# Channel mixer up projection: three 256-column passes into one sum, in place of a 512-column and a 256-column pass

## The chip, the core and the metric

The kernel runs on one core of a Trainium2 chip. The time is the device time of one execution in microseconds; of the kernel before there are three runs, and their median is 1437.25 us (1434.41 to 1437.47). One more execution was recorded by the hardware profiler; the rows quoted below are from it. TensorE multiplies matrices, VectorE (DVE) and ScalarE (ACT) do elementwise work, GpSimd (POOL) some small operations, and the SyncE queue (SP) issues the transfers between HBM and the on-chip memory SBUF. Matmuls write to PSUM, from where VectorE and ScalarE read.

## The reference

One layer of a diffusion backbone works on 256 latent tokens of width 2048 (and 256 context tokens in its first half). After a token mixer with a gated residual comes the channel mixer, and its first half is what is changed here:

```python
def conv_ffn(h, w_up, cw, cb, w_down, grid):
    gate, val = jnp.split(h @ w_up, 2, axis=-1)
    if grid:
        gate = dwconv2d_grid(gate, cw, cb)
    ...
    return (jax.nn.gelu(gate, approximate=False) * val) @ w_down
```

`h` is 256 x 2048, `w_up` 2048 x 11264 (two halves of 5632), `dwconv2d_grid` a depthwise 3x3 convolution over a grid of 4 x 64 tokens. All of it is fp32.

## The kernel before

**Precision in parts.** TensorE is fed numbers in a reduced fp32 format. Each operand is therefore split into a rounded part (hi) and the rest (lo), and a product is summed from hi x hi, hi x lo and lo x hi. A weight block of 128 x 2048 goes through `wtile` (L130 to L141): a transfer into `raw` on the SP queue, a cast on ScalarE into `whi` (L137), and the difference on VectorE into `wlo` (L140). There are three buffers of `raw`, three of `whi`, two of `wlo`. `take` hands out the block that is ready and prepares the next one. The buffers of `whi` and `wlo` are 64 floats longer than a block, and a table `places` says at which float of its buffer each block's two parts start: WIDE 0 and 0, NARROW 16 and 16 (64 bytes), PAIRED 16 for hi and 0 for lo.

**Stages.** First come modulation and the value projection, then eight heads of the token mixer (blocks ff and fb with 512 columns, q, b and a with 256 columns, all through `gemm_w`), eight blocks g, the output projection (wo), the residual and the modulated activations `h2`; then `phase3`, the channel mixer's up stage, and `phase4`, its down projection (dn). In phase 3 there are NFF = 44 values of j; for each there is a gate block and a val block, 88 blocks in all. The weights are the stationary operand (128 x 128 at a time, 16 of them per block, index kb), and the activations are the moving one: `h2` is laid out as [128, 16, 2, 256], so that for each kb the 256 columns of hi and the 256 of lo lie side by side.

**A pair.** For each kb, `mm2_w` (L201 to L207) sends whi over all 512 columns at once: the left half of the PSUM tile gets hi x hi, the right half hi x lo. Then it sends wlo over the 256 columns of hi into the left half. The q, b, a and g blocks use `mm3_w` (L192 to L199) instead: three passes of 256 columns, all into one sum. The first gate block (`late`, L768) has three passes of 256 columns in another order, since parts of h2 become ready only then.

**Behind the matmuls.** `add_parts` (L1140 to L1144) copies the right half from PSUM to SBUF on ScalarE (`low`) and adds the left half on VectorE. For a gate block this gives `g`; ScalarE makes the centre tap and the bias from it (`gacc`, L1151), VectorE adds the eight other taps (L1157), ScalarE applies GELU (`ge`, L1161). For a val block the sum gives `hd`, which is multiplied by `ge` (L1137) and split into `hid_hi` (ScalarE) and `hid_lo` (VectorE, L989) for phase 4.

**Order.** TensorE's instructions stand in the order of the program; those of VectorE and ScalarE are placed by a scheduler by priorities, weights first.

Of the kernel before, what the change touches and what calls it, by code (L numbers as in the profile page):

```python
# [8 lines left out]
F32 = mybir.dt.float32  # L9
# [3 lines left out]
AF = mybir.ActivationFunctionType  # L13
PSUM = bass.MemoryType.PSUM

P = 128
D = 2048
SEQ = 256
DEPTH = 1
HEADS = 8  # L20
# [3 lines left out]
NFF = DFF // P  # L24
KB = D // P
# [17 lines left out]
Y_DG, Y_CX, Y_O, Y_OT, Y_CT = 22, 6.5, 1.5, 6.5, 6  # L43

WBUF = 2048 + 64
WIDE, NARROW, PAIRED = (0, 0), (16, 16), (16, 0)
LEVELS = (1, 2, 4, 8, 16, 32, 64)


# [64 lines left out]
class _Kernel:  # L114
# [83 lines left out]
        nc.tensor.matmul(out, wh, xl, start=False, stop=False)  # L198
        nc.tensor.matmul(out, wl, xh, start=False, stop=stop)  # L199

    def mm2_w(self, ps, hi, lo, x, kb, start, stop):  # L201


        nc = self.nc
        nc.tensor.matmul(ps, hi[:, kb * P:(kb + 1) * P], x, start=start, stop=False, skip_group_check=True)  # L205
        nc.tensor.matmul(ps[:, :SEQ], lo[:, kb * P:(kb + 1) * P], x[:, 0], start=False, stop=stop,  # L206
                         skip_group_check=True)  # L207

    def mm3_x(self, out, hi, lo, xh, xl, kb, start, stop, w=512, tick=True):

        nc = self.nc
        wh = hi[:, kb * w:(kb + 1) * w]
        wl = lo[:, kb * w:(kb + 1) * w]
        nc.tensor.matmul(out, xh, wh, start=start, stop=False)  # L214
        nc.tensor.matmul(out, xh, wl, start=False, stop=False)  # L215
        nc.tensor.matmul(out, xl, wh, start=False, stop=stop)  # L216
        if tick:
            self.tick(w * 3 / 2400)
# [30 lines left out]
    def run(self):  # L249
        tc, nc, a = self.tc, self.nc, self.a  # L250

        def enter(**kw):
            p = tc.tile_pool(**kw)
            return p, p.__enter__()
# [18 lines left out]
        for j in range(NFF):  # L273
            srcs += [a["wup"][0, j], a["wup"][1, j]]
        srcs += [a["wdn"][n, kq] for n in range(4) for kq in range(NFF // 4)]
        places = ([WIDE] * 2 + [NARROW] * 3) * HEADS + [NARROW] * HEADS + [WIDE] * 16 + [PAIRED] * 2 * NFF
        places += [WIDE] * NFF


# [62 lines left out]
        upp, up = enter(name="up", bufs=2, side="right")  # L342
# [412 lines left out]
            nc.scalar.copy(G[:, q * 512:(q + 1) * 512], ps)  # L755


    def gemm_w(self, key, x, n, paired=False, late=False):

        hi, lo = self.take()  # L760
        ps = self.mm_tile(key)
        wk = lambda w, kb: w[:, kb * P:(kb + 1) * P]
        if late:

            for q in range(KB // 4):
                for i, (w, part) in enumerate(((hi, 0), (lo, 0), (hi, 1))):
                    for kb in range(4 * q, 4 * q + 4):
                        self.nc.tensor.matmul(ps[:, part * SEQ:(part + 1) * SEQ], wk(w, kb), x[:, kb, part],  # L768
                                              start=kb == 0 and i == 0, stop=kb == KB - 1 and i > 0,
                                              skip_group_check=True)  # L770
            return ps
        for kb in range(KB):
            if paired:
                self.mm2_w(ps, hi, lo, x[:, kb], kb, kb == 0, kb == KB - 1)
            else:
                self.mm3_w(ps[:, :n], hi, lo, x[:, kb, 0, :n], x[:, kb, 1, :n], kb, kb == 0, kb == KB - 1)
            self.tick(n * 3 / 2400)
        return ps

# [349 lines left out]
    def phase3(self, up):  # L1129
        nc = self.nc  # L1130
        for j in range(NFF):
            ps = self.gemm_w("gate", self.h2, SEQ, True, j == 0)
            ge = self.gate_conv(up, j, ps)
            ps = self.gemm_w("val", self.h2, SEQ, True)
            hd = up.tile([P, SEQ], F32, tag="hd", name="hd")
            self.add_parts(up, hd, ps)
            nc.vector.tensor_mul(hd, hd, ge)  # L1137
            self.split(self.hid_hi[:, j, :], self.hid_lo[:, j, :], hd)

    def add_parts(self, up, out, ps):  # L1140

        low = up.tile([P, SEQ], F32, tag="low", name="low")
        self.nc.scalar.copy(low, ps[:, SEQ:])
        self.nc.vector.tensor_add(out, ps[:, :SEQ], low)  # L1144

    def gate_conv(self, up, j, ps):
        nc = self.nc
        g = up.tile([P, 4, 64], F32, tag="gate", name="gate")
        acc = up.tile([P, 4, 64], F32, tag="gacc3", name="gacc3")
        self.add_parts(up, g.rearrange("p r c -> p (r c)"), ps)  # L1150
        nc.scalar.activation(acc, g, AF.Identity, scale=self.par("fcw", j * 9 + 4), bias=self.par("fcb", j))  # L1151
        taps = [(dy, dx) for dy in (-1, 0, 1) for dx in (-1, 0, 1) if dy or dx]
        for dy, dx in taps:
            r0, r1 = max(0, -dy), min(4, 4 - dy)
            c0, c1 = max(0, -dx), min(64, 64 - dx)
            o = acc[:, r0:r1, c0:c1]
            nc.vector.scalar_tensor_tensor(o, g[:, r0 + dy:r1 + dy, c0 + dx:c1 + dx],  # L1157
                                           self.par("fcw", j * 9 + (dy + 1) * 3 + dx + 1), o,
                                           op0=ALU.mult, op1=ALU.add)
        ge = up.tile([P, SEQ], F32, tag="ge", name="ge")  # L1160
        nc.scalar.activation(ge, acc.rearrange("p r c -> p (r c)"), AF.Gelu)  # L1161
        return ge
# [134 lines left out]
```

## Time and profile before

| | |
|---|---|
| runs, median (three runs) | 1437.25 us (1434.41 to 1437.47) |
| the profiled execution | 1433.68 us |
| its span | 1431.9 us, mean granted clock 0.993 |
| TensorE busy | 1390.7 us (97%) |
| VectorE busy | 1097.4 us (77%) |
| ScalarE busy | 738.1 us (52%) |
| first matmul of the first gate block | 686.5 us |
| first matmul of the first val block | 692.6 us |
| first matmul of the down projection | 1179.8 us |

The table's last three lines bound the up stage: about 493 us of the span. In the profile, a group's row gives line, engine, operation, tiles (written <- read), shape and count, then busy time, the mean duration of one in ns, and idle time of the engine before it. PE stands for TensorE's matmuls, PEld for its weight loads. Matmuls overlap, so a duration isn't the distance from one to the next; that is read from starts in the timeline.

### The profile page before, as it was taken

The numbers are of one execution on the slowest core, as the hardware profiler recorded it, in microseconds if no ns is written. First come the engines' busy times: TensorE is split into PE (matmuls) and PEld (weight loads), VectorE is DVE, ScalarE is ACT, GpSimd is POOL, SyncE is SP. The second block draws the span as 40 slices with busy tenths as digits, with TensorE's granted clock in tenths as the row PEclk, the third lists the DMA queues.
The fourth block names the chain that finished last, engine by engine and source line by source line (L and its number), as shares of the span: only waits on it lengthen the run. The fifth ranks groups of instructions, "written<-read, shape, count | busy, mean of one in ns | idle before, by whom it ended". The sixth has DMA issues, their size and how long they took to land.

```text
span 1431.9 us, 22182 instructions
## 1 busy us (share of the span) xinstructions
PE 1390.7 (97%) x8880; PEld 1179.1 (82%) x8880; DVE 1097.4 (77%) x1665; ACT 738.1 (52%) x1218; POOL 31.2 (2%) x57
## 2 busy tenths in 40 slices
PE   4999999999999999999999999999999999999997
PEld 2566888888888898888888888888888888888886
DVE  3444898899999999776788888888888886667544
ACT  4334456766666676437654545545455543333531
POOL 0000001001000010000000000000000000000000
PEclk8999999999999999999999999999999999999999
DMA  9988676446654665786445545555455558878652
GB/s 370 386 322 332 252 267 232 169 173 224 231 194 160 236 231 216 288 299 260 146 178 191 191 179 195 185 189 194 177 195 187 186 196 311 332 273 318 236 188 105
DMA packets 49143, 329.21 MB, mean 230 GB/s; under 512 B 5392, under 2 KB 5648, under 8 KB 10896
## 3 DMA queue, kind: packets, MB, share of 16 engines
q1 hardware_dynamic: 49040, 327.80, 61.5%
q8 instruction: 69, 1.13, 0.3%
q14 instruction: 34, 0.28, 0.1%
HBM read 323.58 MB, written 4.19 MB: 229 GB/s over the span
## 4 chain that ended last, share of the span: by engine, by line
PE 79%; DVE 10%; ACT 4%; DMA 3%; issue 2%; POOL 1%; SPq 0%; DVEq 0%; POOLq 0%; ACTq 0%
PE val L205 11%; PE gate L205 11%; PE val L206 6%; PE gate L206 6%; PE dn L215 5%; PE dn L214 5%; PE dn L216 5%; DVE wlo L140 3%; PE v L214 2%; PE wo L216 2%; PE wo L214 2%; PE wo L215 2%; DVE acc L942 2%; PE v L216 2%; PE v L215 2%
## 5 line engine op out<-in xcount | busy, mean ns | idle before, releaser
L140 DVE TENSOR_TENSOR wlo<-raw,whi 128x2048 fp32r<-128x2048 f32 x193 | 441.6, 2288 | 104.5 <-PE dn L215 56.1
L137 ACT CAST whi<-raw 128x2048 fp32r<-128x2048 f32 x193 | 369.0, 1912 | 292.7 <-PE val L205 93.6
L205 PE MATMUL val<-h,whi 128*128 128x512 f32 x704 | 248.4, 395 | 0.0
L205 PE MATMUL gate<-h,whi 128*128 128x512 f32 x688 | 242.7, 395 | 0.0
L206 PE MATMUL val<-h,wlo 128*128 128x256 f32 x704 | 197.8, 281 | 0.0
L206 PE MATMUL gate<-h,wlo 128*128 128x256 f32 x688 | 193.3, 281 | 0.0
L1157 DVE SCALAR_TENSOR_TENSOR gacc<-gate,params,gacc 128x189 f32<-128x189 f32 (+2 forms) x352 | 151.4, 430 | 37.3 <-ACT gacc L1151 29.5
L205 PEld LDWEIGHTS val<-h,whi 128*128 128x128 f32 x704 | 132.3, 188 | 29.7
L205 PEld LDWEIGHTS gate<-h,whi 128*128 128x128 f32 x688 | 129.2, 188 | 29.1
L215 PE MATMUL dn<-wlo,hid_hi 128*128 128x512 f32 x352 | 137.1, 389 | 0.6 <-DVE wlo L140 0.6
L214 PE MATMUL dn<-whi,hid_hi 128*128 128x512 f32 x352 | 137.4, 390 | 0.0
L216 PE MATMUL dn<-whi,hid_lo 128*128 128x512 f32 x352 | 137.0, 389 | 0.0
L206 PEld LDWEIGHTS val<-h,wlo 128*128 128x128 f32 x704 | 133.7, 190 | 0.0
L206 PEld LDWEIGHTS gate<-h,wlo 128*128 128x128 f32 x688 | 130.6, 190 | 0.0
L721 DVE SCALAR_TENSOR_TENSOR big<-graw,cs,big 128x1024 f32<-128x1024 f32 x90 | 113.2, 1276 | 11.9 <-DMA graw<-in_wm_dram 11.8
L942 DVE SCALAR_TENSOR_TENSOR acc<-u,params,acc 128x242 f32<-128x242 f32 (+14 forms) x240 | 98.6, 468 | 0.0
L215 PEld LDWEIGHTS dn<-wlo,hid_hi 128*128 128x128 f32 x352 | 66.1, 188 | 14.6 <-DVE wlo L140 1.0
L216 PEld LDWEIGHTS dn<-whi,hid_lo 128*128 128x128 f32 x352 | 66.1, 188 | 13.9
L214 PEld LDWEIGHTS dn<-whi,hid_hi 128*128 128x128 f32 x352 | 66.1, 188 | 13.5
L214 PE MATMUL v<-vw,hT 128*128 128x512 f32 x128 | 53.8, 420 | 4.2 <-ACT hT L988 3.7
L1161 ACT ACTIVATE ge<-gacc 128x256 f32<-128x256 f32 x44 | 18.4, 418 | 74.7 <-DVE gacc L1157 74.7
L197 PE MATMUL fb<-hT,whi 128*128 128x512 f32 x128 | 53.0, 414 | 0.0
(269 smaller groups left out, 2544.7 us busy)
## 6 DMA issues: line engine op xcount, KB each, us to landing
raw<-in_wup_dram SPq DMA_DIRECT2D x88, 1024.0 KB, 4.8
graw<-in_wm_dram SPq DMA_DIRECT2D x64, 1024.0 KB, 5.0
raw<-in_win_dram SPq DMA_DIRECT2D x48, 1024.0 KB, 5.0
raw<-in_wdn_dram SPq DMA_DIRECT2D x44, 1024.0 KB, 4.8
mraw<-in_wm_dram SPq DMA_DIRECT2D x32, 1024.0 KB, 10.0
raw<-in_wout_dram SPq DMA_DIRECT2D x16, 1024.0 KB, 4.9
vraw<-in_wv_dram SPq DMA_DIRECT2D x16, 512.0 KB, 6.5
x<-in_x_dram SPq DMA_DIRECT2D x2, 1024.0 KB, 7.2
```

The lines of the kernel that those rows point to most:

```text
L137: self.nc.scalar.copy(hi, raw)
L140: self.nc.vector.tensor_sub(lo, raw, hi.bitcast(F32))
L197: nc.tensor.matmul(out, wh, xh, start=start, stop=False)
L205: nc.tensor.matmul(ps, hi[:, kb * P:(kb + 1) * P], x, start=start, stop=False, skip_group_check=True)
L206: nc.tensor.matmul(ps[:, :SEQ], lo[:, kb * P:(kb + 1) * P], x[:, 0], start=False, stop=stop, skip_group_check=True)
L214: nc.tensor.matmul(out, xh, wh, start=start, stop=False)
L215: nc.tensor.matmul(out, xh, wl, start=False, stop=False)
L216: nc.tensor.matmul(out, xl, wh, start=False, stop=stop)
L721: nc.vector.scalar_tensor_tensor(self.gacc[:, sl], w[:, sl], c, self.gacc[:, sl], op0=ALU.mult, op1=ALU.add)
L942: nc.vector.scalar_tensor_tensor(d, u[:, lo + o:hi + o], self.par("cw", j * CONVW + k), d, op0=ALU.mult, op1=ALU.add)
L1157: nc.vector.scalar_tensor_tensor(o, g[:, r0 + dy:r1 + dy, c0 + dx:c1 + dx], self.par("fcw", j * 9 + (dy + 1) * 3 + dx + 1), o, op0=ALU.mul ...
L1161: nc.scalar.activation(ge, acc.rearrange("p r c -> p (r c)"), AF.Gelu)
```

## The change

`phase3` no longer uses `mm2_w`, which goes away: each kb of a block has the three passes of `mm3_w`, 256 columns each, into the left half of the PSUM tile alone. `places` has NARROW for the 88 blocks, so that wlo, too, starts 64 bytes into its buffer; whi did before. The late block's passes go into one sum. `add_parts` goes away: ScalarE copies the gate's sum from PSUM into `g` and makes `gacc` from PSUM, and the product with `ge` reads the val sum from PSUM.

```diff
-WIDE, NARROW, PAIRED = (0, 0), (16, 16), (16, 0)
+WIDE, NARROW = (0, 0), (16, 16)
...
-    def mm2_w(self, ps, hi, lo, x, kb, start, stop):
-
-
-        nc = self.nc
-        nc.tensor.matmul(ps, hi[:, kb * P:(kb + 1) * P], x, start=start, stop=False, skip_group_check=True)
-        nc.tensor.matmul(ps[:, :SEQ], lo[:, kb * P:(kb + 1) * P], x[:, 0], start=False, stop=stop,
-                         skip_group_check=True)
...
-        places = ([WIDE] * 2 + [NARROW] * 3) * HEADS + [NARROW] * HEADS + [WIDE] * 16 + [PAIRED] * 2 * NFF
+        places = ([WIDE] * 2 + [NARROW] * 3) * HEADS + [NARROW] * HEADS + [WIDE] * 16 + [NARROW] * 2 * NFF
...
-                        self.nc.tensor.matmul(ps[:, part * SEQ:(part + 1) * SEQ], wk(w, kb), x[:, kb, part],
-                                              start=kb == 0 and i == 0, stop=kb == KB - 1 and i > 0,
-                                              skip_group_check=True)
+                        self.nc.tensor.matmul(ps[:, :n], wk(w, kb), x[:, kb, part], start=kb == 0 and i == 0,
+                                              stop=kb == KB - 1 and i == 2)
...
-            if paired:
-                self.mm2_w(ps, hi, lo, x[:, kb], kb, kb == 0, kb == KB - 1)
-            else:
-                self.mm3_w(ps[:, :n], hi, lo, x[:, kb, 0, :n], x[:, kb, 1, :n], kb, kb == 0, kb == KB - 1)
+            self.mm3_w(ps[:, :n], hi, lo, x[:, kb, 0, :n], x[:, kb, 1, :n], kb, kb == 0, kb == KB - 1)
...
-            self.add_parts(up, hd, ps)
-            nc.vector.tensor_mul(hd, hd, ge)
+            nc.vector.tensor_mul(hd, ps[:, :SEQ], ge)
...
-        self.add_parts(up, g.rearrange("p r c -> p (r c)"), ps)
-        nc.scalar.activation(acc, g, AF.Identity, scale=self.par("fcw", j * 9 + 4), bias=self.par("fcb", j))
+        psv = ps[:, :SEQ].rearrange("p (r c) -> p r c", r=4)
+        nc.scalar.copy(g, psv)
+        nc.scalar.activation(acc, psv, AF.Identity, scale=self.par("fcw", j * 9 + 4), bias=self.par("fcb", j))
```

TensorE's order in a val block before:

```order
L205 MATMUL val<-h_6190,whi 128x512
L206 MATMUL val<-h_6190,wlo 128x256
L205 MATMUL val<-h_6190,whi 128x512
L206 MATMUL val<-h_6190,wlo 128x256
L205 MATMUL val<-h_6190,whi 128x512
```

and with the change (h_6190 is `h2`):

```order
L197 MATMUL val<-h_6190,whi 128x256
L198 MATMUL val<-h_6190,whi 128x256
L199 MATMUL val<-h_6190,wlo 128x256
L197 MATMUL val<-h_6190,whi 128x256
L198 MATMUL val<-h_6190,whi 128x256
```

Two rows per kb become three. The scheduler also places VectorE's work of one j differently. Before, from one gate block's sum to the next (gacc is the accumulator of the taps):

```order
L1144 TENSOR_TENSOR gate<-gate,low 128x256
L1157 SCALAR_TENSOR_TENSOR gacc_7334<-gate,params,gacc_7334 128x3x63
L1157 SCALAR_TENSOR_TENSOR gacc_7334<-gate,params,gacc_7334 128x192
L1157 SCALAR_TENSOR_TENSOR gacc_7334<-gate,params,gacc_7334 128x3x63
L1157 SCALAR_TENSOR_TENSOR gacc_7334<-gate,params,gacc_7334 128x4x63 x2
L1157 SCALAR_TENSOR_TENSOR gacc_7334<-gate,params,gacc_7334 128x3x63
L140 TENSOR_TENSOR wlo<-raw,whi 128x2048
L1157 SCALAR_TENSOR_TENSOR gacc_7334<-gate,params,gacc_7334 128x192
L1144 TENSOR_TENSOR hd<-val,low 128x256
L1157 SCALAR_TENSOR_TENSOR gacc_7334<-gate,params,gacc_7334 128x3x63
L1137 TENSOR_TENSOR hd<-hd,ge 128x256
L989 TENSOR_TENSOR hid_lo<-hd,hid_hi 128x256
```

With the change:

```order
L140 TENSOR_TENSOR wlo<-raw,whi 128x2048
L1139 SCALAR_TENSOR_TENSOR gacc_7415<-gate,params,gacc_7415 128x3x63
L1139 SCALAR_TENSOR_TENSOR gacc_7415<-gate,params,gacc_7415 128x192
L1139 SCALAR_TENSOR_TENSOR gacc_7415<-gate,params,gacc_7415 128x3x63
L1139 SCALAR_TENSOR_TENSOR gacc_7415<-gate,params,gacc_7415 128x4x63 x2
L1139 SCALAR_TENSOR_TENSOR gacc_7415<-gate,params,gacc_7415 128x3x63
L1139 SCALAR_TENSOR_TENSOR gacc_7415<-gate,params,gacc_7415 128x192
L1139 SCALAR_TENSOR_TENSOR gacc_7415<-gate,params,gacc_7415 128x3x63
L140 TENSOR_TENSOR wlo<-raw,whi 128x2048
L1124 TENSOR_TENSOR hd<-val,ge 128x256
L977 TENSOR_TENSOR hid_lo<-hd,hid_hi 128x256
```

The two sums are gone, and the second wlo of a j stands behind all eight taps, ahead of the product with ge, in place of behind the first six.

More of the change, by code (lines that the diff above doesn't have):

```diff
@@ L755, in gate_rows, with gemm_w @@
             nc.scalar.copy(G[:, q * 512:(q + 1) * 512], ps)
-    def gemm_w(self, key, x, n, paired=False, late=False):
+    def gemm_w(self, key, x, n, late=False):
         hi, lo = self.take()
@@ L1131, in phase3 @@
         for j in range(NFF):
-            ps = self.gemm_w("gate", self.h2, SEQ, True, j == 0)
+            ps = self.gemm_w("gate", self.h2, SEQ, j == 0)
             ge = self.gate_conv(up, j, ps)
-            ps = self.gemm_w("val", self.h2, SEQ, True)
+            ps = self.gemm_w("val", self.h2, SEQ)
             hd = up.tile([P, SEQ], F32, tag="hd", name="hd")
-            self.add_parts(up, hd, ps)
-            nc.vector.tensor_mul(hd, hd, ge)
+            nc.vector.tensor_mul(hd, ps[:, :SEQ], ge)
             self.split(self.hid_hi[:, j, :], self.hid_lo[:, j, :], hd)
[L1140 to L1144, printed above, removed]
     def gate_conv(self, up, j, ps):
```

## The prediction

> **What bounds the kernel now.** I read the first line and the engine table first, then the costliest groups, then the order of single matmuls in time.
>
> ```profile
> span 1431.9 us, 22182 instructions
> PE 1390.7 (97%) x8880; PEld 1179.1 (82%) x8880; DVE 1097.4 (77%) x1665; ACT 738.1 (52%) x1218; POOL 31.2 (2%) x57
> L205 PE MATMUL val<-h,whi 128*128 128x512 f32 x704 | 248.4, 395 | 0.0
> L206 PE MATMUL val<-h,wlo 128*128 128x256 f32 x704 | 197.8, 281 | 0.0
> ```
>
> TensorE has no idle time before these groups, so the channel mixer's up stage lasts as long as its matmuls take to follow one another. The mean of one (395 and 281 ns) isn't that: a pair would be 676 ns, 16 pairs 10.8 us. Matmuls overlap, so what counts is start to start, which only the timeline shows. Here are the first matmuls of a val block, of the next gate block and of the next val block (start, duration, operation):
>
> ```profile
> 804.58 0.40 PE L205 MATMUL val<-h,whi 128*128 128x512 f32 x1
> 804.81 0.28 PE L206 MATMUL val<-h,wlo 128*128 128x256 f32 x1
> 804.93 0.39 PE L205 MATMUL val<-h,whi 128*128 128x512 f32 x1
> ...
> 810.18 0.40 PE L205 MATMUL gate<-h,whi 128*128 128x512 f32 x1
> ```
>
> A block is 5.60 us. It has 16 pairs, so a pair is 350 ns: 0.23 us for 512 columns, 0.12 us for 256. The view by windows says the same of two blocks, and that nothing else is short:
>
> ```profile
> core 0: us, PE busy (x) PEld busy (x) DVE busy (x) ACT busy (x) POOL busy (x), PEclk, DMA share, GB/s
> 333.66:339.11 5.45, 5.45 (x51) 5.45 (x49) 5.38 (x8) 3.97 (x6) 0.00 (x0) 1.00 0.92 349
> 181.79:193.09 11.30, 11.30 (x97) 11.30 (x96) 10.64 (x10) 5.83 (x8) 0.00 (x0) 1.00 0.87 321
> 804.58:815.78 11.20, 11.20 (x67) 9.85 (x66) 9.29 (x15) 5.78 (x7) 0.00 (x0) 1.00 0.53 187
> ```
>
> In the last row the clock is full, VectorE is busy 9.29 of 11.20 us, the DMA engines half. All but the first of the 88 blocks run like this.
>
> **The change part by part.**
>
> *TensorE.* 87 blocks of 16 pairs (1392 pairs) become 1392 triples of 256 columns: the same 768 columns, three weight loads for two. The price of such a triple need not be guessed: the token mixer's q, a, b and g go through the same helper (L197 to L199), with 256 columns, and their weights already lie 64 bytes into the buffers. An undisturbed block of 48 matmuls, a of the fifth head, and the start of what follows:
>
> ```profile
> 333.67 0.28 PE L197 MATMUL a<-hT,whi 128*128 128x256 f32 x1
> ...
> 339.11 0.40 PE L197 MATMUL ff<-hT,whi 128*128 128x512 f32 x1
> ```
>
> That is 5.44 us, 113.3 ns a matmul, 340 ns a triple. Two other blocks, q and b of the first head, also without a gap, are slower:
>
> ```profile
> 181.79 0.28 PE L197 MATMUL q<-hT,whi 128*128 128x256 f32 x1
> ...
> 187.44 0.28 PE L197 MATMUL b<-hT,whi 128*128 128x256 f32 x1
> ...
> 193.10 0.28 PE L197 MATMUL a<-hT,whi 128*128 128x256 f32 x1
> ```
>
> 11.31 us for two: 5.655 us a block, 117.8 ns a matmul, 353.4 ns a triple. So the stream has two steady spacings, about 4.5 ns apart, and the up stage gets one of them or a mixture. The bounds for 87 blocks are therefore 87 x (5.44 - 5.60) = -13.9 us and 87 x (5.655 - 5.60) = +4.8 us. The recorded duration tells the two apart, and the groups say which is common:
>
> ```profile
> L198 PE MATMUL a<-hT,whi 128*128 128x256 f32 x128 | 35.4, 276 | 0.0
> L198 PE MATMUL q<-hT,whi 128*128 128x256 f32 x128 | 35.6, 278 | 0.0
> L214 PE MATMUL dn<-whi,hid_hi 128*128 128x512 f32 x352 | 137.4, 390 | 0.0
> ```
>
> 276 ns belongs to the fast spacing; the pair's 256-column matmul has 281. All of a has 276 in the mean; q and b have 278, two fifths of the way to 281, and they are the blocks into which other work is pushed. So most of these streams settle on the fast spacing, those with the fewest interruptions above all, and the up stage has none. The paired stream itself sits on the slow side (395 against 390 ns in dn, 281 against 276), which I put down to its two alternating widths and weight offsets: after the change both are uniform, as in a. I take 5.44 us.
>
> Is there a fixed cost per matmul, which three would pay once more than two? Two of a's matmuls take 2 x 113.3 = 227 ns. One of 512 columns in the last stage, start to start:
>
> ```profile
> 1250.11 0.39 PE L214 MATMUL dn<-whi,hid_hi 128*128 128x512 f32 x1
> 1250.34 0.39 PE L215 MATMUL dn<-wlo,hid_hi 128*128 128x512 f32 x1
> 1250.56 0.39 PE L216 MATMUL dn<-whi,hid_lo 128*128 128x512 f32 x1
> ```
>
> 0.45 us for two, so 225 ns to the rounding: on the fast side no fixed cost shows, on the slow side some 4 to 5 ns (353.4 - 350 for one matmul more). [...]
>
> *The weights' place.* Only wlo moves, by 64 bytes. The first gate block (the late one) has three passes of 256 already and partly waits for h2; its 16 wlo matmuls could gain some ns each. Bounds 0 and -0.2 us; I take -0.1.
>
> *ScalarE and VectorE.* Per j go two ScalarE copies (one becomes the copy into g) and two VectorE sums; the product with ge reads PSUM. That work lies beside TensorE, which never waits for it, so removing it is worth nothing by itself (were TensorE faster than the chain, two sums of 0.42 us per j). But the chain through both engines has a period too, and TensorE is about to ask for 10.88 us (2 x 5.44) in place of 11.20:
>
> ```profile
> 804.78 2.29 DVE L140 TENSOR_TENSOR wlo<-raw,whi 128x2048 fp32r<-128x2048 f32 x1
> 806.99 0.42 DVE L1144 TENSOR_TENSOR gate<-gate,low 128x256 f32<-128x256 f32 x1
> 808.08 2.80 DVE L1157 SCALAR_TENSOR_TENSOR gacc<-gate,params,gacc 128x189 f32<-128x189 f32 x6 [0.67 <-ACT gacc L1151]
> 810.79 2.29 DVE L140 TENSOR_TENSOR wlo<-raw,whi 128x2048 fp32r<-128x2048 f32 x1
> ...
> 815.50 0.42 DVE L989 TENSOR_TENSOR hid_lo<-hd,hid_hi 128x256 fp32r<-128x256 f32 x1 [0.47 <-ACT hid_hi L988]
> 815.98 2.29 DVE L140 TENSOR_TENSOR wlo<-raw,whi 128x2048 fp32r<-128x2048 f32 x1
> ```
>
> ```profile
> 806.48 0.36 ACT L1143 COPY low<-gate 128x256 f32<-128x256 f32 x1
> 807.44 0.60 ACT L1151 ACTIVATE gacc<-gate,params 128x256 f32<-128x256 f32 x1 [0.60 <-DVE gate L1144]
> 815.07 0.41 ACT L988 CAST hid_hi<-hd 128x256 fp32r<-128x256 f32 x1 [0.49 <-DVE hd L1137]
> ```
>
> From 804.78 to 815.92 VectorE's chain has 0.06 us to spare; unchanged, it would hold TensorE at about 11.15 us. After the change, counted from the gate block's end (804.58): copy at +1.90, gacc straight behind it +2.26 to +2.86 (its 0.60 us wait for the sum is gone); eight chained taps at 2.80/6 = 0.467 us, to +6.6; wlo of the next val to +8.9; the product with ge 0.42, hid_hi 0.41 and hid_lo 0.42 with their hand-overs of 0.05, to +10.3. The next wlo can't begin before its buffer is free at 10.88 + 0.20. So 0.8 us are spare: the chain follows. If a read from PSUM took twice its 0.4 to 0.6 us, the spare would be gone and the period would be some 11.1. The weights move in VectorE's order to behind all eight taps, but are ready at +8.9 for a block that starts at +10.88: 2 us of cover. For the casts of whi and the loads:
>
> ```profile
> ACT whi L137 <- PE val L205: 93.6, 43, 2.2
> ```
>
> ScalarE's cast waits for TensorE to free a buffer, 2.2 us each time, not for the load, and 0.53 of the DMA time in use becomes 0.55. In the SP queue one load of the residual moves behind one weight load of the next stage. It is wanted only at the very end; were it in the way, it would cost at most one landing:
>
> ```profile
> raw<-in_wdn_dram SPq DMA_DIRECT2D x44, 1024.0 KB, 4.8
> ```
>
> *Sum*: -13.9 - 0.1 = -14.0 us against the profiled execution, 1433.68 us (span 1431.9), so 1419.7. The runs shown have a median of 1437.25, 3.6 above it, and the two others are 1434.41 and 1437.47. The step is the same in each, so I forecast 1437.25 - 14.0 = **1423**.
>
> **The rivals.**
>
> *Slow spacing throughout (slower).* The up stage's stream enters on the 117.8 ns side and stays there, as q and b of the first head did for 96 matmuls. Then the third weight load and matmul cost what they save and more: 87 x 0.055 = +4.8 us, **1442**. For it: the paired stream is on that side from the first val block to the last, in the same tiles, and nothing interrupts the stage to bring it off. Against: the blocks of a, and q's and b's after most interruptions, return to 276 ns. It decides where the mean spacing exceeds 350/3 = 116.7 ns. That the spacing has a fixed cost per matmul is the same rival, and its chance is the one below. [...]
>
> *Mixture.* Gaps or block boundaries throw the stream between the two, as in q and b: at 278 ns, two fifths slow, a matmul takes 113.3 + 0.4 x 4.5 = 115.1 ns, a triple 345.3, so 1392 x -4.7 ns = -6.5 us, **1431**. Against: the up stage has no other work pushed in.
>
> *VectorE becomes the bound.* If PSUM reads stretch the chain to its old 11.15 us, 44 x 0.05 = -2 us, **1435**. For it: 0.06 us of slack now. Against: 0.8 us by the count above.
>
> **How the numbers follow.** Fast spacing 0.64, slow throughout 0.15, mixture 0.13, VectorE 0.06, anything else 0.02. The likeliest alone would be 1419 to 1427 (the runs lie 3.06 us apart, the bounds of the small terms add 1). For 8 in 10 the range must take in the mixture and VectorE's case as well: 1418 to 1438, which leaves out the slow case and the ends. A measurement here can tell about 0.2% (2.9 us) from no change: faster 0.77 (fast, mixture), same 0.07, slower 0.16.
>
> **What would show it.** Right: start to start 113 ns and a duration of 276 ns in the gate and val groups, three lines (L197 to L199) of about 1392 matmuls in place of two, blocks of 5.44 us, PEld busy all the time, no idle before them; dn would begin about 14 us sooner. The slow rival shows 281 ns and blocks of 5.65; the mixture a mean between; VectorE as bound shows idle time or short gaps before a block's first wlo matmul, released by wlo's line. What makes the prediction wrong is a spacing in h2's stream that differs from hT's: that step carries the whole sum.

## The result, and the profile after

| | before | after |
|---|---|---|
| median | 1436.33 us (1434.41 to 1437.47, four runs) | **1421.74 us** (1419.87 to 1425.92, four runs) |
| ratio | | 0.9904, 95% interval 0.9878 to 0.993 |
| profiled execution, span | 1431.9 us | 1418.1 us (1419.87 us with what lies around it) |

The forecast was 1423 us with a range of 1418 to 1438. The page of the kernel after, its span and three (those of val; gate's are alike) of the six groups that take the place of the four before:

```profile
span 1418.1 us, 24793 instructions
PE 1375.5 (97%) x10272; PEld 1224.9 (86%) x10272; DVE 1073.3 (76%) x1577; ACT 716.6 (51%) x1174; POOL 31.2 (2%) x57
...
L199 PE MATMUL val<-h,wlo 128*128 128x256 f32 x704 | 194.3, 276 | 0.0
L197 PE MATMUL val<-h,whi 128*128 128x256 f32 x704 | 194.3, 276 | 0.0
L198 PE MATMUL val<-h,whi 128*128 128x256 f32 x704 | 194.3, 276 | 0.0
```

There are 1392 matmuls more, and each of the six groups has a mean duration of 276 ns: the fast side. The timeline gives the starts of two successive blocks, and the view by windows the whole stage from its first val block to the down projection, after and (second fence) before. A row of that view has the window, its sum, the busy time of PE, PEld, DVE, ACT and POOL with their instructions, the granted clock, the DMA share and GB/s:

```profile
781.04 0.28 PE L197 MATMUL val<-h,whi 128*128 128x256 f32 x1
...
786.48 0.28 PE L197 MATMUL gate<-h,whi 128*128 128x256 f32 x1
...
694.00:1167.28 473.28, 473.28 (x4178) 473.28 (x4177) 379.50 (x523) 230.88 (x262) 0.00 (x0) 1.00 0.55 193
```

```profile
692.58:1179.78 487.20, 487.20 (x2787) 428.42 (x2786) 403.15 (x609) 252.20 (x305) 0.00 (x0) 1.00 0.52 187
```

5.44 us a block, 473.28 against 487.20 us for the stage: 13.92 us less. The rest of the span almost cancels. The stage began 1.42 us later than before (694.00 against 692.58), although the late block itself took 0.09 us less (5.99 against 6.08): in the token mixer, q, b and a (L198) have a mean of 279 ns in this execution against 278, 278 and 276, more of their blocks being on the slow side. Executions differ by more than that: the first gate block of the stage begins between 686.5 and 691.2 us in the eleven profiled executions of this document whose tiles ahead of the stage lie at the same places. After the stage, the down projection is 1.32 us shorter; a wait of 0.6 us for a wlo in it is gone. -13.92 + 1.42 - 1.32 = -13.82, the difference of the spans.

VectorE's chain in the kernel after (one j, from the end of a gate block at 781.04):

```profile
781.24 2.29 DVE L140 TENSOR_TENSOR wlo<-raw,whi 128x2048 fp32r<-128x2048 f32 x1 [1.16 <-PE gate L199]
783.80 3.71 DVE L1139 SCALAR_TENSOR_TENSOR gacc<-gate,params,gacc 128x189 f32<-128x189 f32 x8 [0.27 <-ACT gacc L1133]
787.43 2.29 DVE L140 TENSOR_TENSOR wlo<-raw,whi 128x2048 fp32r<-128x2048 f32 x1
789.63 0.42 DVE L1124 TENSOR_TENSOR hd<-val,ge 128x256 f32<-128x256 f32 x1
790.52 0.42 DVE L977 TENSOR_TENSOR hid_lo<-hd,hid_hi 128x256 fp32r<-128x256 f32 x1 [0.47 <-ACT hid_hi L976]
792.12 2.29 DVE L140 TENSOR_TENSOR wlo<-raw,whi 128x2048 fp32r<-128x2048 f32 x1 [1.17 <-PE gate L199]
```

It now waits 1.17 us of each 10.88 for TensorE to free a buffer.

### The profile page after: what moved, and what is told of

It reads as the page before. It is cut to its first block, busy times and chain, and to the rows that moved or that the text cites. A ratio compares the mean times of both kernels' runs of the same rounds, so it can differ in the third digit from the quotient of the medians.

```text
span 1418.1 us, 24793 instructions
## 1 busy us (share of the span) xinstructions
PE 1375.5 (97%) x10272; PEld 1224.9 (86%) x10272; DVE 1073.3 (76%) x1577; ACT 716.6 (51%) x1174; POOL 31.2 (2%) x57
## 4 chain that ended last, share of the span: by engine, by line
PE 77%; DVE 11%; ACT 4%; DMA 3%; issue 2%; POOL 2%; SPq 0%; DVEq 0%; POOLq 0%; ACTq 0%
PE val L197 6%; PE val L199 6%; PE val L198 6%; PE dn L206 6%; PE gate L197 6%; PE dn L208 6%; PE gate L199 5%; PE dn L207 5%; PE gate L198 5%; DVE wlo L140 3%; DVE acc L930 3%; PE v L206 2%; PE wo L208 2%; PE wo L206 2%; PE wo L207 2%
## 5 line engine op out<-in xcount | busy, mean ns | idle before, releaser
L199 PE MATMUL val<-h,wlo 128*128 128x256 f32 x704 | 194.3, 276 | 0.0
L197 PE MATMUL val<-h,whi 128*128 128x256 f32 x704 | 194.3, 276 | 0.0
L198 PE MATMUL val<-h,whi 128*128 128x256 f32 x704 | 194.3, 276 | 0.0
L197 PE MATMUL gate<-h,whi 128*128 128x256 f32 x688 | 189.9, 276 | 0.0
L198 PE MATMUL gate<-h,whi 128*128 128x256 f32 x688 | 189.9, 276 | 0.0
L199 PE MATMUL gate<-h,wlo 128*128 128x256 f32 x688 | 189.9, 276 | 0.0
L197 PEld LDWEIGHTS val<-h,whi 128*128 128x128 f32 x704 | 132.2, 188 | 0.0
L198 PEld LDWEIGHTS val<-h,whi 128*128 128x128 f32 x704 | 132.2, 188 | 0.0
L197 PEld LDWEIGHTS gate<-h,whi 128*128 128x128 f32 x688 | 129.1, 188 | 0.0
L198 PEld LDWEIGHTS gate<-h,whi 128*128 128x128 f32 x688 | 129.1, 188 | 0.0
L713 DVE SCALAR_TENSOR_TENSOR big<-graw,cs,big 128x1024 f32<-128x1024 f32 x90 | 113.5, 1278 | 14.0 <-DMA graw<-in_wm_dram 13.9
L208 PEld LDWEIGHTS dn<-whi,hid_lo 128*128 128x128 f32 x352 | 66.1, 188 | 13.9
```

Of the source, the lines that this page charges most:

```text
L197: nc.tensor.matmul(out, wh, xh, start=start, stop=False)
L713: nc.vector.scalar_tensor_tensor(self.gacc[:, sl], w[:, sl], c, self.gacc[:, sl], op0=ALU.mult, op1=ALU.add)
```

## The experiments

The theory on trial: a triple takes 340 ns because the weights that are loaded lie 64 bytes off from the columns that stream, in a uniform stream; such a stream can also run on a slow side, at 353 ns, and takes one of the two when it starts. The rivals: a spacing that belongs to three uniform passes wherever their weights lie; a gain that comes from the removed copies and sums; a fast side that is the only lasting one. All but the last run are single executions with a profile; the kernel before, run beside them on the same chip, took 1435.74, 1440.53 and 1435.38 us in the three groups.

### The weights' place, with triples

```diff
-        places = ... + [WIDE] * 16 + [NARROW] * 2 * NFF
+        places = ... + [WIDE] * 16 + [WIDE] * 2 * NFF
```

> The changed kernel with both weight parts of the 88 up blocks at byte 0 of their buffers in place of byte 64. Theory (the triple is fast because of where its weights lie): the one place in the trace of before where 256-column passes load weights from byte 0 is the late block's wlo, 0.48 us for four, 120 ns each; a triple is then 360 ns, a block 5.76 us, the stage 28 us longer, about 1450 us. Rival (the spacing is a property of three uniform 256-column passes, wherever the weights lie): 113 ns, 5.44 us a block, 1422 us.

It took 1450.15 us. A block is 5.76 us, and the spacing is exactly 120 ns for all three passes:

```profile
800.12 0.28 PE L197 MATMUL val<-h,whi 128*128 128x256 f32 x1
...
805.88 0.28 PE L197 MATMUL gate<-h,whi 128*128 128x256 f32 x1
```

The rival falls. Triples with both parts at byte 0 lose some 14 us against the kernel before; 64 bytes are worth 28 us. (The kernel before had whi at byte 64 and only wlo at byte 0; triples with these two places were not run.)

```diff
+        places = ... + [WIDE] * 16 + [(24, 24)] * 2 * NFF
```

> The changed kernel with both weight parts of the up blocks at byte 96 of their buffers in place of 64; h2 stays. The distance to h2 is 96 modulo 128. Theory of the distance: something between 113 ns (64) and 120 ns (0), the same as with h2 moved so that the distance is 32; about 1436 us. If any place but byte 0 does: 113 ns, 1422 us.

1443.33 us, blocks of 5.69 to 5.70 us, spacings between 115 and 122 ns with a mean of 118.7. Byte 96 is nearly as bad as byte 0.

### The weights' place, with pairs

In the kernel before, PAIRED becomes (16, 16) in one run and (0, 0) in the other:

> The kernel before with wlo, too, 64 bytes into its buffer; the pairs stay. Theory in the prediction's form (two weight offsets in turn keep the paired stream on the slow side): a pair falls from 350 to 340 ns, a block to 5.44 us, about 1422 us, and the change's gain would come from the weights' place alone. Rival (two widths in turn, or the 512-column pass with weights at byte 64, keep it slow): 350 ns or more, 1436 us or more.

> The kernel before with whi, too, at byte 0; the pairs stay. Theory as for the pair at 64 bytes (one offset for all): 340 ns, 1422 us. Rival (what counts is that a load which runs beside a 256-column pass starts at byte 64, here it no longer does): 350 ns or slower, up to 360, 1436 to 1450 us.

1438.53 and 1441.25 us, the difference being ahead of the stage. Blocks of 5.65 and 5.65 to 5.66 us, here at byte 64:

```profile
795.35 0.40 PE L205 MATMUL val<-h,whi 128*128 128x512 f32 x1
...
801.00 0.40 PE L205 MATMUL gate<-h,whi 128*128 128x512 f32 x1
```

The theory's part on offsets falls: with one offset for both parts a pair is slower (353 ns), not faster, than with two (350). The mean of a 512-column pass is 397 ns at byte 64 and 399 at byte 0, against 395 in the kernel before and 390 in dn. Start to start, the two passes of a pair take 232.1 and 117.9 ns in the mean in the kernel before, 235.0 and 118.3 at byte 64, 236.5 and 116.9 at byte 0, where 226.8 (dn) and 113.3 (a) are the fast spacings of the two widths; with those a pair would take 340 ns, as the triple does. So of the three placements tried none lets a pair keep the fast spacing; that the two widths in turn are the cause fits, but was not isolated.

### Triples, but with the copies and sums kept

The kernel before with PAIRED (16, 16), and in `mm2_w`:

```diff
-        nc.tensor.matmul(ps, hi[:, kb * P:(kb + 1) * P], x, start=start, stop=False, skip_group_check=True)
+        nc.tensor.matmul(ps[:, :SEQ], wh, x[:, 0], start=start, stop=False, skip_group_check=True)
+        nc.tensor.matmul(ps[:, SEQ:], wh, x[:, 1], start=False, stop=stop, skip_group_check=True)
```

> Three passes of 256 columns, weights at byte 64, but hi x lo into the right half of the PSUM tile, so that the ScalarE copies and VectorE sums stay. It tells the matmuls' part of the gain from that of the work removed. If the removed work only lay beside TensorE: 1422 us, blocks of 5.44 us. If VectorE's chain of 11.15 us per gate and val block, which the trace of before shows, becomes the bound: 44 x (11.15 - 10.88) = 12 us more, 1434 us, with idle time ahead of a block's wlo matmuls.

1434.26 us: the expected time, but not in the expected way. TensorE isn't held to the chain's pace. The first 22 blocks after the late one take 5.44 us. VectorE's chain takes 11.06 us per j (here from 805.95 to 817.01) and falls 0.18 us further behind with each 10.88, until its cover of about 2 us is used up. Then a wlo comes late, once:

```profile
805.95 2.29 DVE L140 TENSOR_TENSOR wlo<-raw,whi 128x2048 fp32r<-128x2048 f32 x1
...
811.95 2.29 DVE L140 TENSOR_TENSOR wlo<-raw,whi 128x2048 fp32r<-128x2048 f32 x1
...
817.01 2.29 DVE L140 TENSOR_TENSOR wlo<-raw,whi 128x2048 fp32r<-128x2048 f32 x1
```

```profile
808.57 0.28 PE L206 MATMUL gate<-h,whi 128*128 128x256 f32 x1
...
814.01 0.28 PE L206 MATMUL val<-h,whi 128*128 128x256 f32 x1
814.12 0.28 PE L207 MATMUL val<-h,whi 128*128 128x256 f32 x1
814.30 0.39 PE L208 MATMUL val<-h,wlo 128*128 128x256 f32 x1
...
819.82 0.28 PE L206 MATMUL gate<-h,whi 128*128 128x256 f32 x1
...
825.47 0.28 PE L206 MATMUL val<-h,whi 128*128 128x256 f32 x1
```

The wlo begun at 811.95 ends at 814.24, and the third matmul at 814, the first that needs it, starts 0.18 us after the second in place of 0.11, and from there on the stream is on the slow side: 5.65 us a block for the remaining 64, in which 11.3 us per j leave VectorE time enough, so no further wait comes to change it. What followed a wait of under 0.1 us cost 64 x 0.21 = 13 us. So the sums did hide beside TensorE in the kernel before, and still the whole gain needs their removal: a chain of 11.06 us per j can't keep up with 10.88.

### What puts a stream on one side or the other

Ten extra matmuls of 512 columns (over h2's kb 0, its hi and lo columns), ahead of the gate block at j = 4, 8, ..., 40:

```diff
+            if j and j % 4 == 0:
+                self.nc.tensor.matmul(self.ax_tile("kick"), self.hid_hi[:, 0, 0:P],
+                                      self.h2[:, 0].rearrange("p i t -> p (i t)"), start=True, stop=True)
```

> The changed kernel with one matmul of 512 columns more ahead of the gate block at j = 4, 8, ..., 40 (ten in all, 0.23 us each, 2.3 us; its result is used by nothing). It asks what makes the stream change sides. Theory (either spacing holds until something else comes between, and then a side is taken anew): some of the eleven stretches of 8 blocks run at 113 ns, some at 118 ns; each slow one costs 8 x 0.21 = 1.7 us. If about a fifth are slow, as in q, a, b and g of the trace of before: 1422 + 2 + 4 = 1428 us. Rival (in this stage the fast spacing is the only lasting one): all stretches return to 113 ns within some matmuls, 1424 us.

1422.48 us, as the rival had it. All ten stretches were back at 113 ns within three matmuls; they had also been at 113 ns ahead of each kick. Ten waits instead, by writing a wlo three or four times:

```diff
+            if i in LATE:
+                for _ in range(LATE[i]):
+                    self.nc.vector.tensor_sub(lo, raw, hi.bitcast(F32))
```

> The changed kernel with the wlo of the gate block made late at j = 4, 8, ..., 40: VectorE writes the same difference three or four times (2.3 us each), so that TensorE has to wait at the first wlo matmul of that block. It asks whether a wait can put the stream on the slow side. The waits themselves cost, by 0.2 + 3 x 2.29 - 5.44 = 1.6 us or 3.9 us, and once more some 0.5 to 3 us at the next val block, 10 x 4 = 40 us or so, about 1460 us; what counts is the spacing after them. Theory (a stream takes a side anew after a wait and keeps it): some of the ten stretches of 7 to 8 blocks at 118 ns (blocks of 5.65 us), the others at 113 ns. Rival (the stage returns to 113 ns after any interruption within a block): all blocks without a wait 5.44 us.

1478.4 us. The long waits cost more than I had priced: in the one shown first, TensorE stood idle for 6.0 us rather than 3.9, and the mean granted clock over the block was 0.76; its matmuls had a mean of 351 to 367 ns in place of 278, and it took 14.4 us in place of 5.44. The two windows are a block with a long and one with a short wait:

```profile
735.30:749.70 14.40, 8.42 (x50) 8.23 (x49) 10.07 (x12) 2.72 (x3) 0.00 (x0) 0.76 0.40 146
789.30:796.40 7.10, 5.75 (x50) 5.55 (x49) 6.88 (x9) 1.90 (x1) 0.00 (x0) 1.00 0.60 227
```

After two of the ten waits (both long) the stream was slow, for seven blocks of 5.65 us each, until the next wait, after which it was fast again; after the other eight it was fast, 5.44. Block starts from the first slow stretch and from the fast one that follows:

```profile
778.01 0.28 PE L201 MATMUL gate<-h,whi 128*128 128x256 f32 x1
...
783.67 0.28 PE L201 MATMUL val<-h,whi 128*128 128x256 f32 x1
```

```profile
807.30 0.28 PE L201 MATMUL val<-h,whi 128*128 128x256 f32 x1
...
812.74 0.28 PE L201 MATMUL gate<-h,whi 128*128 128x256 f32 x1
```

The same waits with a kick two j after each:

> The same late weights, and two j after each the matmul of 512 columns of the kick run. Theory (a single pass of another width brings a stream from the slow to the fast side): stretches that are slow after a wait are at 113 ns from the kick on, so every second half of a stretch has blocks of 5.44 us. Rival (it takes a side at random, or the kick leaves a slow stream alone): slow stretches go on past the kick.

1475.2 us, and a piece of luck: this execution entered the up stage on the slow side, without any change there. It ran slow through the first wait until the first kick, and fast from there:

```profile
698.46:732.40 33.94, 33.94 (x291) 33.94 (x290) 26.79 (x34) 17.20 (x19) 0.00 (x0) 1.00 0.47 162
751.86:763.16 11.30, 11.30 (x98) 11.30 (x97) 8.71 (x13) 5.27 (x6) 0.00 (x0) 1.00 0.53 189
768.85:779.70 10.85, 10.85 (x98) 10.85 (x97) 8.71 (x12) 5.27 (x6) 0.00 (x0) 1.00 0.53 187
```

Six blocks in 33.94 us and two in 11.30 are 5.65 us each; after the kick at 763.21 two take 10.88 (the window, cut a little short, has 10.85). The other nine waits and kicks left it fast. So both sides last for tens of microseconds, and in this stage the stream changed sides only at a wait or a kick. After all 20 kicks it was fast, but ahead of 19 it had been fast already: one case from the slow side is few. And a pass of another width isn't enough by itself. In the token mixer, q of the first head follows fb's 48 passes of 512 columns without a gap. In 12 of the 14 profiled executions it is slow from its start (the two others are a run in which one wlo buffer lies elsewhere and one in which fb's weights do, both below). In the kernel before:

```profile
181.56 0.39 PE L199 MATMUL fb<-hT,wlo 128*128 128x512 f32 x1
181.79 0.28 PE L197 MATMUL q<-hT,whi 128*128 128x256 f32 x1
...
187.44 0.28 PE L197 MATMUL b<-hT,whi 128*128 128x256 f32 x1
```

That is 5.65 us for q's block. What chooses the side is not known.

### Where the streaming columns start

h2 96 bytes lower, with room made first by shorter wlo buffers, then by fewer 4-byte columns in the residual:

```diff
-        self.h2 = h2.tile([P, KB, 2, SEQ], F32R, name="h2")
+        self.h2 = h2.tile([P, KB * 2 * SEQ + 24], F32R, name="h2")[:, :KB * 2 * SEQ].rearrange(
+            "p (k i t) -> p k i t", k=KB, i=2)
```

> The changed kernel with the moving operand h2 96 bytes lower: in the built program whi, wlo, hT and h2 all start 96 bytes past a multiple of 128, now h2 starts at a multiple, and the weights stay at byte 64 of their buffers (their distance to h2, modulo 128 bytes, goes from 64 to 32). Theory (what counts is the distance between the weights that are being loaded and the columns that stream): the spacing leaves 113 ns, towards the 120 ns of distance 0, so 117 ns or so, blocks of 5.6 us, about 1436 us. Rival (what counts is the weights' own address): 113 ns, 1422 us. If the rate of the stream itself hangs on where its columns start, it could also fall below 113.

> The changed kernel with h2 96 bytes lower, as in the run before with h2 moved, but with all buffers of whi and wlo where they were (the place is taken from some 4-byte columns in the residual). In the earlier run the second wlo buffer had moved by 128 bytes as well, and its blocks were irregular. Theory (the distance between loaded weights and streaming columns decides): far from 113 ns again, 117 to 120 ns, 1440 to 1452 us. Rival (the moved wlo buffer was the cause): 113 ns, 1422 us.

1454.03 and 1450.05 us. The first is spoilt by the second wlo buffer, which had moved by 128 bytes: its blocks differ from one another (5.75 to 5.82 us). Such a move leaves every distance modulo 128 as it was, so that isn't all that counts. The second has even blocks of 5.76 us, a mean spacing of 120 ns made of 115 to 125:

```profile
800.00 0.29 PE L197 MATMUL val<-h,whi 128*128 128x256 f32 x1
...
805.76 0.29 PE L197 MATMUL gate<-h,whi 128*128 128x256 f32 x1
```

The weights had not moved, yet the fast spacing was gone, so their own address isn't all that decides. (In both runs the stage's small tiles, gate, gacc3, ge and hd, move by 96 bytes too; TensorE reads none of them.) Distances of 0, 32 and 96 bytes (modulo 128) gave 120, 120 and 118.7 ns, 64 gave 113.3. Moving both by the same amount would show whether only the distance counts; it was not tried.

The same question for the blocks of 512 columns:

```diff
-        places = ([WIDE] * 2 + [NARROW] * 3) * HEADS + [NARROW] * HEADS + [WIDE] * 16 + [NARROW] * 2 * NFF
-        places += [WIDE] * NFF
+        places = ([(8, 8)] * 2 + [NARROW] * 3) * HEADS + [NARROW] * HEADS + [(24, 24)] * 16 + [NARROW] * 2 * NFF
+        places += [(8, 8)] * NFF
```

> The changed kernel with other places for the blocks of 512 columns: ff, fb and dn at byte 32 of their buffers, wo at byte 96 (in place of 0). In dn and wo the weights are the moving operand, so that it starts at a multiple of 128 (dn) or 64 bytes past one (wo); in ff and fb they are the loaded one. [...] Rival (227 ns is the stream's rate wherever it starts): no change in dn, wo, ff and fb, 1422 us, or slower if byte 0 was the best place.

1432.13 us: slower, what the rival had for the case that byte 0 was the best place. In dn, where the weights are the columns that stream:

```profile
L206 PE MATMUL dn<-whi,hid_hi 128*128 128x512 f32 x352 | 139.5, 396 | 0.0
```

396 ns against 390, and start to start 233.3 against 226.8 in the mean; 1056 of them are 6.9 us. wo, ff and fb went from about 227 to 232 or 233. The up stage was untouched (473.28 us). So 227 ns for 512 columns and 113.3 for 256 are the best that any place tried has given.

### A kick at the entry

```diff
+            if j == 0:
+                self.nc.tensor.matmul(self.ax_tile("kick"), self.h2[:, 0, 0, 0:P],
+                                      self.h2[:, 0].rearrange("p i t -> p (i t)"), start=True, stop=True)
             ps = self.gemm_w("val", self.h2, SEQ)
```

> The changed kernel with one matmul of 512 columns between the late gate block and the first val block, and nothing else. Theory (this pass puts the stream on the fast side whichever side the late block left it on): the profiled execution has all of the 87 later blocks at 5.44 us, and no execution of the up stage is slow, so that the runs lie closer together than those of the changed kernel (1419.87 to 1425.92); the median is 0.2 us above that kernel's at most, 1420 to 1423 us, and below it if some of its executions enter slowly. Rival (the side is taken at random, kick or not): the same median, and now and then a run 19 us longer.

1420.02 us (1418.98 to 1420.97, four runs) against 1436.35 for the kernel before beside it; ratio 0.9887, 95% interval 0.987 to 0.9903. The intervals of this and of the change overlap, so it isn't shown to be faster than the change; its runs lie 2.0 us apart, those of the change 6.1. All 87 blocks of the profiled execution were fast, but the late block's last matmuls, ahead of the kick, were 113 ns apart already, so the kick had nothing to mend there. Whether it guards against an entry like the one above is not shown.

## Why the prediction was right

- **The price of a triple (87 x -0.16 = -13.9 us).** It came out as 13.92. The row that priced it, a block of the same helper with the same width and place, was the right one because it matched in all that the runs found to matter: 256 columns throughout, weights at byte 64, streams that start at the same offset (in the built program hT and h2 both start 96 bytes past a multiple of 128). The means of 395 and 281 ns would have given nothing of this: the duration of a pass was longer in the pair, but the gain lies in its start-to-start times.
- **The two sides of the spacing (bounds -13.9 and +4.8 us).** Both are real in the up stage itself. But the reason given for the fast side, that the streams with the fewest interruptions settle there, was wrong. The prediction's own q and b of the first head run 96 matmuls without a gap on the slow side. And a, of which all eight blocks ended fast in the trace of before, ended slow in five of eight in the execution of the kernel after, on the same code. That the stage entered on the fast side was likely, but luck in so far as nothing in the prediction settles it. The slow rival, 0.15, had the right mechanism; one execution of the six with triples at byte 64 and no kick at the entry took that side there (113 ns: the change, the two sums, the ten kicks, the wide places, the late weights; 118: the late weights with kicks).
- **Why the pair was slow.** This step failed in half. The pair did sit on the slow side, with both of its passes (232.1 and 117.9 ns). I put that down to two widths and two weight offsets in turn; with one offset, at byte 64 or at 0, a pair took 353 ns, more than 350. Why it is slow stays open.
- **The mixture rival.** Block boundaries didn't throw the stream: within a stretch of the up stage (blocks of 5.44 or of 5.65 us throughout) no block changed sides unless a wait, or a pass of another width, came between.
- **No fixed cost per matmul.** 113.3 ns for 256 columns and 226.8 for 512 held in the stage after and in dn. On the slow side two passes of 256 take 3.5 ns more than one of 512 (2 x 117.8 against 232.1); the prediction's own difference, 353.4 - 350, is 3.4 and not the 4 to 5 that it says. In the stage, the triple is 10 ns faster than the pair, with one matmul more (340 against 350).
- **VectorE and ScalarE.** I counted hid_lo's end at +10.3 us and 0.8 us to spare; it ended at 790.94, +9.9, with 1.17 us of waiting. Reads from PSUM took no longer than those from SBUF (gacc 0.57 us against 0.60 before, the product with ge 0.42 in both): gacc's taps began at 783.80, +2.76, where I had counted +2.86. The remark that an unchanged chain "would hold TensorE at about 11.15 us" was wrong in its mechanism: the chain does lag, but 2 us of cover let TensorE run ahead for 22 blocks, and what then cost the time was the slow side, on which the stream was from one short wait on.
- **The late block** gained 0.09 us, as taken (0.1).
- **Not foreseen**: 1.4 us lost ahead of the stage, which the change doesn't touch and which lies within the spread of executions, and 1.3 us regained in the down projection. That they cancelled is luck.

## What to carry to other kernels

Price a new stream of matmuls by start-to-start times of a stream that already runs with the same width, the same helper and the same byte offsets, not by durations and not by counting matmuls: here three passes beat two by 3% of the stage, and lost 3% when their weights lay 64 bytes elsewhere. When TensorE gets faster, compare the period of the engines beside it with its new one: work that was hidden at 11.20 us per j wasn't at 10.88. And when a stage's time differs in steps of a few per cent between executions, look whether its whole stream sits at another spacing (here 5.44 or 5.65 us a block) before looking for waits.

## What the runs showed of the hardware that was not expected

- In this kernel the spacing of uniform 256-column passes hung on where the weights that are loaded and the columns that stream start. By their byte distance modulo 128 it was 113.3 ns at 64, 120 at 0, 120 at 32 and 118.7 at 96; that the distance alone counts is not shown. A move of the weights alone by 64 bytes made a difference of 6% (120 against 113.3); what causes it is not shown.
- The uniform stream had a fast and a slow steady spacing (113.3 and 117.8 ns at the same place). A wait of under 0.1 us was followed by the slow one for 64 blocks. After 20 made waits the stream was slow three times (once it had been slow already), and two waits took it from slow to fast. After 20 single passes of 512 columns it was never slow; right behind the 48 of the first head's fb it was slow in 12 of 14 executions.
- Place mattered for 512 columns, too: 226.8 ns with the weights at byte 0, 232 to 233 at byte 32 or 96.
